# Two more output blocks ahead of the last retention head's scores, and two blocks of h read from PSUM at the end

## The chip, the core and the metric

The kernel runs on one core of a Trainium2 chip. The core has five engines with a queue of instructions each: TensorE (PE in the profile; its weight loads are shown apart as PEld), VectorE (DVE), ScalarE (ACT), GpSimd (POOL) and SyncE (SP), which here issues every transfer. An engine takes its queue in order; engines wait for each other by semaphores. The metric is device time in microseconds (us), the median over several executions.

## The reference

The reference is a decoder trunk with two layers over x of 1024 tokens x 1024 channels in fp32.

- Layer 0: `u = rms_norm(h)`; one projection gives q, k (4 heads x 256), v and a gate g (4 heads x 512). q and k are rotated. Retention runs in chunks of 128 tokens: per head `o = (q k^T * decay) v + (q * decay) state`, and `state = state * decay + (k * decay)^T v`. Each head's o is normalized over its 512 channels, multiplied by `silu(g)` and projected by `ret_w_out` (2048 to 1024). `h = x + rms_norm(y)`.
- Between the layers: `rms_norm(h) @ w_kv` gives one shared K (8 heads x 128) and V (8 heads x 256).
- Layer 1: q and gate from a projection of `rms_norm(h)`; stick-breaking attention (for each query, weights `sigmoid(z) * prod(1 - sigmoid(z))` over the later keys) over the shared K and V; gate, output projection, and again `h = h + rms_norm(y)`. The result is h.

## The kernel before

Activations lie transposed, channels on the 128 partitions and tokens along the free axis, in halves of 512 tokens, t=0 and t=1. Every fp32 matmul runs as three passes of a reduced fp32 form (`mm3`, L415 high by high, L416 high by low, L417 low by high). So each operand is first split: ACT writes the high part (L577, or L580 with a gain) and DVE the low part (L578, L581). Weights come by transfers into `wraw` (or other free tiles: `vo`, `ko`) and are split into `whl`, which has three buffers.

`run()` (L1493 to L1588) emits four phases in order: retention for t=0 and t=1 (class AHead, four heads u=0 to 3 each), then stick-breaking attention for t=0 and t=1 (CPair, four pairs of heads each), and `finish` at the end. A head of retention goes: projection of q and k; output projection of the head before (`last.out(yd)`, function `outproj`); scores (`H.scores()`); projection of v and g (`H.vg()`); and then, mixed into the next head's work, the product with v, normalization (L933 to L952), gate product (L979), transposes on PE (L983) and the split into `oT`, for the last head into `qk`.

The output projection is a list of 16 half chunks: eight blocks of 128 output channels, two halves each, 12 matmuls of 512 columns in a block. A block's sum goes to PSUM, DVE adds the sum so far (L517), and a transfer stores it to `y`. `go` and `merge` interleave such lists. For the last head (u=3) `run()` takes the first four half chunks ahead of the scores and holds the other twelve (`held`) to be emitted beside the head's tail. Its four first blocks use the PSUM tag `ma` alone.

PSUM has eight banks under the tags `ma`, `mb`, `z` and `o`, two buffers each. `banks4` (L390) is the usual alternation: ma, ma, mb, mb.

Within an engine the order is not that of the code. A planner (`arrange`, L101 to L305) takes the emitted steps with their reads and writes, and modelled costs, and orders each engine's queue anew. Two sets of a step bind it: `s.before`, steps of any engine that have to be planned earlier, and `s.behind`, the last reader on the same engine.

`finish` writes the last half (t=1) in two parts of 256 tokens, th=0 and th=1. `chunk` does a block: 12 matmuls, DVE adds the sum so far (L1442), ACT squares (L1444) and scales (L1445), DVE adds the square to `acc` (L1447). The last block's square stays in `box["q"]`. Then `col` sums over channels by matmuls with a column of `mean` (L1454, L1455), and POOL raises to the power -1/2 (L1458); `row` spreads the result over the partitions (L1464); `write` multiplies two blocks at once (L1470, k=0 to 3), adds h from the SBUF tile `A` (L1471) and stores. The additions of th=0 and the first of th=1 are on POOL, the three others of th=1 on DVE.

Of the kernel before, what the change touches and what calls it, by code (L numbers as in the profile page):

```python
# [15 lines left out]
AF = mybir.ActivationFunctionType  # L16
ALU = mybir.AluOpType
# [83 lines left out]
def arrange(nc, tc, tag_of, bufs, banks, turns):  # L101

    chip = Step()
    chip.banks = banks
    steps, last, users = [], defaultdict(list), defaultdict(list)
    for ins in nc.cur_bb.bb.instructions:
        s = Step()
        s.ins = [a.bass_ap for a in ins.ins if getattr(a, "bass_ap", None) is not None]
        s.outs = [a.bass_ap for a in ins.outs if getattr(a, "bass_ap", None) is not None]
        s.eng = str(ins.engine).split(".")[-1]  # L110
        if not s.outs or s.eng not in HAND:
            continue
        s.inst, s.op, s.k = ins, type(ins).__name__, len(steps)
        s.scan = bool(getattr(ins, "is_tensor_tensor_scan", False))
        s.turns = bool(getattr(ins, "is_transpose", False))
        s.before, s.after, s.behind, s.next = set(), set(), set(), set()
        reads = [(b.tensor.name, _cells(b)) for b in s.ins if type(b.tensor).__name__ == "Tile"]
        writes = [(b.tensor.name, _cells(b)) for b in s.outs if type(b.tensor).__name__ == "Tile"]
        for name, m in reads:
            s.before |= {o.k for o, n, w in last[name] if w and n & m}  # L120
            s.behind |= set([o.k for o, n, w in last[name] if not w and n & m and o.eng == s.eng][-1:])
        for name, m in writes:
            s.before |= {o.k for o, n, w in last[name] if n & m}
        for name, m in reads:
            last[name].append((s, m, False))
        for name, m in writes:
            last[name] = [z for z in last[name] if z[1] & ~m] + [(s, m, True)]
        s.tiles = sorted({name for name, _ in reads + writes})
        for name in s.tiles:
            users[name].append(s)  # L130
        s.before.discard(s.k)
        s.behind -= s.before | {s.k}
        for p in s.before:
            steps[p].after.add(s.k)
        for p in s.behind:
            steps[p].next.add(s.k)
        s.busy, s.whole = _time(s, chip)
        s.shares = s.eng == "Pool" or s.eng == "DVE" and sum(b.tensor.name not in banks for b in s.ins) > 1
        steps.append(s)
    at = {s.inst.name: s for s in steps}  # L140
    for a, z in turns:
        at[z].behind.add(at[a].k)
        at[a].next.add(at[z].k)
    tags = defaultdict(list)
    for name in sorted((n for n in users if n in tag_of), key=lambda n: users[n][0].k):
        tags[tag_of[name]].append(name)

    rank, best = latest(steps, users, tags, bufs), None
    for _ in range(5):
        end, order, follow = place(steps, users, tags, tag_of, bufs, rank)  # L150
        if best is None or end < best[0]:
            best = end, order
        rank = justify(steps, order, follow)
    order = best[1]
    edge = mybir.DependencyInfo(mybir.DependencyClass.NoSync, mybir.DependencyReason.DATA)
    for line in order.values():
        for a, b in zip(line, line[1:]):
            tc.add_manual_dep(steps[b].inst, steps[a].inst.name, edge, reason="order of the queue")
# [150 lines left out]
def trunk(ctx, tc, xT, wts, gains, trig, ident_in, cols, out):  # L309
# [11 lines left out]
    cnt, tag_of, banks, turns = [0], {}, set(), []  # L321
# [1091 lines left out]
    def finish(t, P, y_d):  # L1413
# [36 lines left out]
        def col(th):  # L1450
            p = PS("z")
            for b in range(2):
                o = 256 * th + 128 * b
                MM(p[:, b:b + 1], acc[:, o:o + 128], mean[:, 0:1], start=True, stop=False)  # L1454
                MM(p[:, b:b + 1], box["q"][:, 128 * b:128 * b + 128], mean[:, 0:1], start=False, stop=True)  # L1455
            ms, r = S("small", [2]), S("col", [4])
            V.tensor_scalar(ms[:], p[:, 0:2], EPS, None, ALU.add)
            G.tensor_tensor(r[:, 0:2], ms[:], mhalf[:, 0:2], ALU.pow)  # L1458
            box["r"] = r
# [6 lines left out]
        def write(th, k):  # L1466
            tl = slice(256 * th, 256 * th + 256)
            yy = f[:, 2 * k:2 * k + 2, tl]
            h = hs[k][:].rearrange("p (c t) -> p c t", c=2)[:, :, tl]
            V.tensor_tensor(yy, yy, box["row"][:, :256].unsqueeze(1).broadcast_to([128, 2, 256]), ALU.mult)  # L1470
            (G if th == 0 or k == 0 else V).tensor_tensor(yy, yy, h, ALU.add)  # L1471
            dma(out[256 * k:256 * k + 256, HT * t + 256 * th:HT * t + 256 * th + 256].rearrange("(c p) t -> p c t", c=2), yy)

        def post(th):
# [18 lines left out]
    def run():  # L1493
# [12 lines left out]
        for ip, (kind, t) in enumerate(phases):  # L1506
# [5 lines left out]
            for u in range(4):  # L1512
                ring[:] = rings(kind, t, u)
                if kind == "A":
                    H = AHead(t, u, X)
                    if u == 0 and ip == 0:
                        main = H.first_v(first)
                        load[0]()
                        for k in range(8):
                            main[2 * k]()  # L1520
                            if k == 0:
                                late_constants()
                            for n in load[3 * k + 1:3 * k + 4]:
                                n()
                            main[2 * k + 1]()
                            if k > 2:
                                norm[k - 3]()
                        go(H.qk(), lambda: [(norm[5:], 0, 4)])
                        go(H.first_g(), lambda H=H: [(H.scores(), 6, 0), (sums, 0, 6)])
                        H.nmix = 0  # L1530
                        last = H
                        continue
                    elif u == 0:
                        go(H.qk())
                    else:
                        n = 7 if ip == 0 and u == 1 else 8
                        go(H.qk(), lambda L=last, n=n: [(L.rest(), 0, n), (L.gate(), 18 - n, 2)])
                        held = last.out(yd, None, None if u < 3 else ("ma",) * 4)
                        go(held if u < 3 else held[:4],
                           lambda H=H, L=last, u=u, side=(pre if u == 2 and nxt[0] == "A" else post[:5] if u == 1 else post[7:10] if u == 2 else pre, 0, 2 if u < 3 else 0):  # L1540
                           [(L.give, 0, 12 if u < 3 else 0), side, (H.scores(), 5, 1) if u < 3 else ([], 0, 0)])
                        held = held[4:]
                    H.nmix = 3 if t else 2
                    go(H.vg(), lambda H=H, u=u, more=post[5:7] if u == 1 else post[10:] if u == 2 else []:
                       [([], 0, 0) if 0 < u < 3 else (H.scores(), 3, 15), (H.begin(), 20, 0), (more, 4, 8)])
                    last = H
# [111 lines left out]
```

## Time and profile before

| | |
|---|---|
| three executions | 1715.61, 1715.69, 1717.03 us; median 1715.69 |
| the profiled execution | 1716.91 us, its span 1714.8 us |
| PE busy | 1700.1 us, 99% of the span, 8057 matmuls |
| DVE, ACT, POOL busy | 1308.4, 880.9, 142.8 us |
| transfers | 348.78 MB, 203 GB/s on average |

The times in the profile's rows count from the start of the span, in us. A timeline row has start, duration, engine, line, operation, what it writes and reads, shapes, and in brackets how long the engine had been idle before, with the instruction that released it; `x4` is a run of four alike. Matmuls are pipelined: the distance of two starts, not the duration, is what a matmul costs. A row of windows has the stretch, its length, and the busy time of PE, weight loads, DVE, ACT and POOL, each with its count, then the granted clock of TensorE (1.00 is full), the share of the DMA engines and GB/s. A row of waits has the waiting engine, tile and line, what it waited for, and total, count and longest wait in us.

### The profile page before, as it was taken

To read this page: it belongs to the slowest core of one execution; us is meant where nothing else is said; L and a number is where in the kernel's file an instruction comes from. 1 tells how busy PE (TensorE), PEld (TensorE's weight loads), DVE (VectorE), ACT (ScalarE), POOL (GpSimd) and SP (SyncE) were. 2 spreads that over 40 slices of the span, in tenths; PEclk is the share of its full clock that TensorE was granted. 3 is DMA by queue.
4 is the path that set the end of the run, shared out by engine and by line. 5 is a ranking of instruction groups with operands and counts; after the bars stand their busy time and mean duration, and the time that the engine had idled before them with its cause. 6 is when DMAs were issued, how large, how long until landed. Compare 5 with 4: busy or idle time off the path is not lost.

```text
span 1714.8 us, 23975 instructions
## 1 busy us (share of the span) xinstructions
PE 1700.1 (99%) x8057; PEld 1419.0 (83%) x8057; DVE 1308.4 (76%) x2213; ACT 880.9 (51%) x1646; POOL 142.8 (8%) x275
## 2 busy tenths in 40 slices
PE   9999999999999999999999999999999999999997
PEld 7888888888888888878888888888888888888887
DVE  8856868889867978688888778667887756656865
ACT  6435536555545535355655544544674445445643
POOL 0000101010010000101010100000001001001001
PEclk9999999999999999999999999999999999999999
DMA  5236475668545676376896999667883763463523
GB/s 187 98 105 203 148 236 185 203 193 271 187 146 176 225 240 209 98 256 209 291 320 198 332 314 308 209 209 257 280 292 111 252 225 101 160 219 99 162 95 125
DMA packets 182250, 348.78 MB, mean 203 GB/s; under 512 B 20208, under 2 KB 24432, under 8 KB 182128
## 3 DMA queue, kind: packets, MB, share of 16 engines
q1 hardware_dynamic: 182128, 347.26, 61.0%
q8 instruction: 63, 1.03, 0.2%
q14 instruction: 59, 0.48, 0.1%
HBM read 273.78 MB, written 73.40 MB: 202 GB/s over the span
## 4 chain that ended last, share of the span: by engine, by line
PE 99%; DMA 0%; DVE 0%; ACT 0%; issue 0%; SPq 0%; POOL 0%; DVEq 0%
PE pmb L415 13%; PE pmb L417 13%; PE pmb L416 13%; PE pma L415 12%; PE pma L417 12%; PE pma L416 12%; PE po L417 5%; PE po L416 5%; PE po L415 5%; PE pz L1355 2%; PE pz L417 2%; PE pz L416 2%; PE pz L415 2%; PE pz L983 1%; PE pz L551 0%; DMA S<-in_xT_dram 0%
## 5 line engine op out<-in xcount | busy, mean ns | idle before, releaser
L577 ACT ACTIVATE whl<-wraw 128x512 fp32r<-128x512 f32 x323 | 190.8, 625 | 203.4 <-PE pmb L417 80.4
L578 DVE TENSOR_TENSOR whl<-wraw,whl 128x512 fp32r<-128x512 f32 x323 | 214.3, 686 | 64.3 <-ACT whl L577 63.1
L415 PE MATMUL pma<-xh,whl 128*128 128x512 f32 x384 | 153.1, 399 | 0.0
L415 PE MATMUL pmb<-xh,whl 128*128 128x512 f32 x384 | 152.4, 397 | 0.0
L417 PE MATMUL pma<-xh,whl 128*128 128x512 f32 x384 | 150.1, 391 | 0.0
L417 PE MATMUL pmb<-xh,whl 128*128 128x512 f32 x384 | 150.0, 391 | 0.0
L416 PE MATMUL pma<-xh,whl 128*128 128x512 f32 x384 | 149.9, 390 | 0.0
L416 PE MATMUL pmb<-xh,whl 128*128 128x512 f32 x384 | 149.6, 390 | 0.0
L1325 DVE TENSOR_TENSOR_SCAN sgn<-sgn 128x384 f32<-128x384 f32 (+4 forms) x64 | 86.5, 1354 | 27.7 <-POOL sgn L1323 27.7
L580 ACT ACTIVATE whl<-wraw,gn 128x256 fp32r<-128x256 f32 (+1 forms) x144 | 80.4, 600 | 50.0 <-PE pmb L417 32.4
L577 ACT ACTIVATE AT<-pz 128x512 fp32r<-128x512 f32 (+1 forms) x96 | 46.3, 487 | 108.0 <-PE pz L1355 105.9
L1322 POOL TENSOR_SCALAR_AFFINE_SELECT A<-A 128x128 f32<-128x128 f32 x64 | 33.1, 516 | 775.1 <-ACT A L1317 775.1
L578 DVE TENSOR_TENSOR AT<-pz,AT 128x512 fp32r<-128x512 f32 (+1 forms) x96 | 52.9, 555 | 57.6 <-ACT AT L577 57.1
L581 DVE SCALAR_TENSOR_TENSOR whl<-wraw,gn,whl 128x256 fp32r<-128x256 f32 (+1 forms) x144 | 82.0, 601 | 17.1 <-ACT whl L580 16.5
L415 PE MATMUL pmb<-oT,whl 128*128 128x512 f32 x240 | 94.9, 396 | 0.0
L417 PE MATMUL pmb<-oT,whl 128*128 128x512 f32 x240 | 93.8, 391 | 0.0
L416 PE MATMUL pmb<-oT,whl 128*128 128x512 f32 x240 | 93.7, 391 | 0.0
L577 ACT ACTIVATE whl<-S 128x512 fp32r<-128x512 f32 x104 | 63.0, 628 | 48.1 <-PE pmb L417 12.5
L417 PEld LDWEIGHTS pmb<-xh,whl 128*128 128x128 f32 x384 | 72.1, 188 | 15.8
L417 PEld LDWEIGHTS pma<-xh,whl 128*128 128x128 f32 x384 | 72.1, 188 | 15.6
L416 PEld LDWEIGHTS pmb<-xh,whl 128*128 128x128 f32 x384 | 72.2, 188 | 13.5
L415 PEld LDWEIGHTS pmb<-xh,whl 128*128 128x128 f32 x384 | 72.2, 188 | 13.4
(389 smaller groups left out, 4614.0 us busy)
## 6 DMA issues: line engine op xcount, KB each, us to landing
wraw<-in_wts_dram SPq DMA_DIRECT2D x522, 256.0 KB, 3.6
y<-f SPq DMA_DIRECT2D x120, 256.0 KB, 3.2
f<-y SPq DMA_DIRECT2D x88, 256.0 KB, 4.1
S<-in_wts_dram SPq DMA_DIRECT2D x44, 256.0 KB, 4.1
vo<-in_wts_dram SPq DMA_DIRECT2D x42, 256.0 KB, 4.3
ko<-in_wts_dram SPq DMA_DIRECT2D x40, 256.0 KB, 4.4
T<-AT SPq DMA_DIRECT2D x32, 256.0 KB, 4.7
sc<-T SPq DMA_DIRECT2D x16, 512.0 KB, 5.1
```

Of the source, the lines that this page charges most:

```text
L415: MM(p, lh, rh, start=start, stop=False, **kw)
L416: MM(p, lh, rl, start=False, stop=False, **kw)
L417: MM(p, ll, rh, start=False, stop=stop, **kw)
L577: A_.activation(dst[0], src, AF.Copy)
L578: V.tensor_tensor(dst[1], src, f32(dst[0]), ALU.subtract)
L580: A_.activation(dst[0], src, AF.Copy, scale=scale)
L581: V.scalar_tensor_tensor(dst[1], src, scale, f32(dst[0]), ALU.mult, ALU.subtract)
L983: nc.tensor.transpose(pt[:, 128 * e:128 * e + 128], on[:, 128 * e:128 * e + 128], ident[:])
L1322: first = G.affine_select(a[:, dg], a[:, dg], [[-1, 128]], ALU.is_gt, 0.0, base=0, channel_multiplier=1)
L1325: V.tensor_tensor_scan(n[:, :W][:, ::-1], n[:, :W][:, ::-1], n[:, :W][:, ::-1], 1.0, ALU.mult, ALU.bypass)
L1355: nc.tensor.transpose(p[:, 128 * tb:128 * tb + 128], self.A[hh][tb][:, c0:c0 + 128], ident[:])
```

## The change

There are four edits. In `arrange`, a read of a PSUM bank is also put behind the reads of that bank by other engines. For the last head, the output projection uses the usual alternation of banks, and eight half chunks instead of four are emitted ahead of the scores, for t=0 and t=1. In `finish`, `col` sums both columns over `acc` first and then both over `box["q"]`, as one accumulation; for th=1, two ACT copies bring the blocks k=2 and k=3 of h to two PSUM banks. In `write`, those two additions read h from PSUM, and POOL does three additions of th=0 (k=0 to 2) and two of th=1 (k=0, 1); the others are DVE's.

```diff
@@ -117,7 +117,7 @@  (arrange)
         for name, m in reads:
-            s.before |= {o.k for o, n, w in last[name] if w and n & m}
+            s.before |= {o.k for o, n, w in last[name] if n & m and (w or name in banks and o.eng != s.eng)}
             s.behind |= set([o.k for o, n, w in last[name] if not w and n & m and o.eng == s.eng][-1:])
@@ -1451,8 +1451,14 @@  (finish, col)
             p = PS("z")
             for b in range(2):
                 o = 256 * th + 128 * b
-                MM(p[:, b:b + 1], acc[:, o:o + 128], mean[:, 0:1], start=True, stop=False)
-                MM(p[:, b:b + 1], box["q"][:, 128 * b:128 * b + 128], mean[:, 0:1], start=False, stop=True)
+                MM(p[:, b:b + 1], acc[:, o:o + 128], mean[:, 0:1], start=b == 0, stop=False, skip_group_check=True)
+            for b in range(2):
+                MM(p[:, b:b + 1], box["q"][:, 128 * b:128 * b + 128], mean[:, 0:1], start=False, stop=b == 1, skip_group_check=True)
+            if th:
+                for k in (2, 3):
+                    box[k] = PS("ma")
+                    A_.activation(box[k][:].rearrange("p (c t) -> p c t", c=2),
+                                  hs[k][:].rearrange("p (c t) -> p c t", c=2)[:, :, 256:512], AF.Copy)
@@ -1468,7 +1474,9 @@  (finish, write)
             V.tensor_tensor(yy, yy, box["row"][:, :256].unsqueeze(1).broadcast_to([128, 2, 256]), ALU.mult)
-            (G if th == 0 or k == 0 else V).tensor_tensor(yy, yy, h, ALU.add)
+            if th and k > 1:
+                h = box[k][:].rearrange("p (c t) -> p c t", c=2)
+            (G if k < (2 if th else 3) else V).tensor_tensor(yy, yy, h, ALU.add)
@@ -1535,11 +1543,11 @@  (run)
-                        held = last.out(yd, None, None if u < 3 else ("ma",) * 4)
-                        go(held if u < 3 else held[:4],
+                        held = last.out(yd)
+                        go(held if u < 3 else held[:8],
...
-                        held = held[4:]
+                        held = held[8:]
```

The edits move instructions in the queues. The names in the rows are tiles with a number for each allocation; the sign <- stands between what is written and what is read, and brackets name the engines waited for. First PE's queue ahead of the scores of the last retention head, t=1. The scores are the matmuls into `pz` from `qk`; `pma`, `pmb` from `oT` are output blocks, L569 spreads a row of norm factors over the partitions, matmuls from `xh` belong to the projection of v and g. Before:

```order
L417 MATMUL pma_7094<-oT_6787,whl_7011 128x512
L569 MATMUL pz_7111<-sgn_7067,onesr 128x512 [waits DVE_49,PE_49]
L569 MATMUL pz_7111<-sgn_7067,onesr 128x512 [waits DVE_49]
L415 MATMUL pz_7187<-qk_6988 128x512 [waits PE_49,Activation_49]
L416 MATMUL pz_7187<-qk_6988 128x512 [waits DVE_49]
```

And with the change, where the first row is the end of the fourth block, and 36 matmuls of the projection stand from the fourth to the fifth of these rows:

```order
L417 MATMUL pmb_7137<-oT_6787,whl_7067 128x512
L569 MATMUL pz_7154<-sgn_7093,onesr 128x512 [waits DVE_49,PE_49]
L569 MATMUL pz_7154<-sgn_7093,onesr 128x512 [waits DVE_49]
L415 MATMUL pma_7168<-whl_7119,xh_3837 128x512 [waits DVE_49,Activation_49]
...
L417 MATMUL po_7217<-whl_7182,xh_3953 128x512
L415 MATMUL pz_7230<-qk_6988 128x512 [waits PE_49]
L416 MATMUL pz_7230<-qk_6988 128x512
```

The scores have moved behind more matmuls, and their waits for ACT and DVE are no longer written at these rows.

Second, PE's queue at the end of retention, t=1: the last transposes (L983) of the gated head, and the first matmul that reads the split of them (`qk`). Before:

```order
L417 MATMUL pma_7734<-oT_6787,whl_7624 128x512
L983 MATMUL pz_7760<-ident,sgn_7672 128x128 [waits DVE_49,PE_49]
L983 MATMUL pz_7760<-ident,sgn_7672 128x128 x3
L415 MATMUL pmb_7767<-oT_6787,whl_7725 128x512
...
L417 MATMUL pmb_7797<-oT_6787,whl_7725 128x512
L415 MATMUL pma_7815<-qk_7578,whl_7788 128x512 [waits Activation_49]
L416 MATMUL pma_7815<-qk_7578,whl_7788 128x512 [waits DVE_49]
```

With the change:

```order
L417 MATMUL pmb_7797<-oT_6787,whl_7705 128x512
L983 MATMUL pz_7757<-ident,sgn_7697 128x128 [waits DVE_49,PE_49]
L983 MATMUL pz_7757<-ident,sgn_7697 128x128 x3
L415 MATMUL pma_7815<-qk_7621,whl_7788 128x512 [waits Activation_49]
L416 MATMUL pma_7815<-qk_7621,whl_7788 128x512 [waits DVE_49]
```

The 24 matmuls of two output blocks that stood between the transposes and the readers are now ahead of the transposes or of the scores. On ACT the high part of these transposes has, with the change, this row of a weight copy in front of it:

```order
L952 ACTIVATE sgn_7697<-po_7667,small_7693,small_7692 128x512 [waits Pool_49]
L577 ACTIVATE whl_7896<-ko_7897 128x512 [waits DMAHW0_49,PE_49,Activation_49]
L577 ACTIVATE qk_7621<-pz_7757 128x4x128 [waits PE_49]
```

Before, a weight copy (`whl_7838<-vo_7839`, waiting for PE) stood there too; it is another one now.

Third, DVE's queue at the end. Before:

```order
L1442 TENSOR_TENSOR oT_16045<-pmb_16570,oT_16045 128x256 [waits PE_49]
L1442 TENSOR_TENSOR oT_16045<-pmb_16591,oT_16045 128x256 [waits PE_49]
L1447 TENSOR_TENSOR acc_16044<-acc_16044,f_16584 128x256 [waits Activation_49]
L1457 TENSOR_SCALAR small_16613<-pz_16608 128x2 [waits PE_49]
...
L1471 TENSOR_TENSOR oT_16045<-oT_16045,A_16171 128x2x256 [waits DVE_49]
L1471 TENSOR_TENSOR oT_16045<-oT_16045,A_16236 128x2x256 [waits DVE_49]
L1471 TENSOR_TENSOR oT_16045<-oT_16045,A_16292 128x2x256 [waits DMAHW4_49,DVE_49]
```

With the change (its lines 1463 and 1479 are 1457 and 1471 of before):

```order
L1442 TENSOR_TENSOR oT_16045<-pmb_16570,oT_16045 128x256 [waits PE_49]
L1479 TENSOR_TENSOR oT_16045<-oT_16045,A_16292 128x2x256 [waits DMAHW4_49,DVE_49]
L1447 TENSOR_TENSOR acc_16044<-acc_16044,f_16584 128x256 [waits Activation_49]
L1442 TENSOR_TENSOR oT_16045<-pmb_16591,oT_16045 128x256 [waits PE_49]
L1463 TENSOR_SCALAR small_16617<-pz_16608 128x2 [waits PE_49]
...
L1479 TENSOR_TENSOR oT_16045<-oT_16045,pma_16613 128x2x256 [waits DVE_49]
L1479 TENSOR_TENSOR oT_16045<-oT_16045,pma_16615 128x2x256 [waits DVE_49]
```

One addition of the first part now stands between the last two evacuations, the last addition to `acc` ahead of the last evacuation, and two additions of three are left at the end, from PSUM.

## The prediction

> **What bounds the kernel now.** I read the page first, then the list of TensorE's waits, then the timeline at each wait, then the granted clock by windows.
>
> ```profile
> span 1714.8 us, 23975 instructions
> PE 1700.1 (99%) x8057; PEld 1419.0 (83%) x8057; DVE 1308.4 (76%) x2213; ACT 880.9 (51%) x1646; POOL 142.8 (8%) x275
> PE 99%; DMA 0%; DVE 0%; ACT 0%; issue 0%; SPq 0%; POOL 0%; DVEq 0%
> ```
>
> TensorE (PE) is busy for 99% of the span, and 99% of the chain that ended last is PE. The change takes no matmul away, so it can only gain where PE stands still or after PE's last matmul. The whole list of PE's waits is five rows, engine and line, then what was waited for, total, count and longest in us:
>
> ```profile
> PE pz L415 <- ACT qk L577: 1.8, 1, 1.8
> PE pz L388 <- DVE f L386: 1.7, 1, 1.7
> PE pma L415 <- ACT oT L580: 1.2, 1, 1.2
> PE pz L1464 <- POOL col L1458: 1.0, 1, 1.0
> PE pz L1454 <- DVE acc L1447: 0.9, 1, 0.9
> ```
>
> Rows two and three are the start of the kernel, which the change does not touch. Rows four and five are in the end stage. Row one is the place of the first edit: the scores of the last retention head, second half of the sequence (t=1). The timeline there:
>
> ```profile
> 728.28 0.39 PE L417 MATMUL pma<-oT,whl 128*128 128x512 f32 x1
> ...
> 729.64 0.40 PE L417 MATMUL pma<-oT,whl 128*128 128x512 f32 x1
> 729.88 0.63 PE L569 MATMUL pz<-sgn,onesr 128*128 128x512 f32 x2
> ...
> 731.66 1.14 ACT L577 ACTIVATE qk<-f 128x512 fp32r<-128x512 f32 x2
> ...
> 732.33 0.50 PE L415 MATMUL pz<-qk 128*128 128x512 f32 x1 [1.82 <-ACT qk L577]
> ...
> 733.06 0.50 PE L417 MATMUL pz<-qk 128*128 128x512 f32 x1
> ...
> 734.17 0.52 PE L415 MATMUL pz<-qk 128*128 128x384 f32 x1
> ...
> 737.45 0.40 PE L416 MATMUL pma<-whl,xh 128*128 128x512 f32 x1
> ```
>
> The held output blocks end at 729.64, and PE stands until the high part of the rotated q and k is written. Between 728.28 and 729.64 lie six starts, so a 512-wide matmul takes 1.36/6 = 0.227 us of PE at full clock; a 384-wide one takes three quarters by width, 0.17. From 729.64 to 737.45 PE starts 13 wide and 5 narrow ones: 13 x 0.227 + 5 x 0.17 = 3.8 us of work in 7.81 us. So this place costs 4.0 us. Waiting alone does not make that up. Each row below is a window, its length, busy time of PE, weight loads, DVE, ACT and POOL, the granted clock, DMA share and GB/s; the first one is the third wait of the list:
>
> ```profile
> 6.94:10.36 3.42, 2.21 (x10) 1.34 (x9) 1.52 (x3) 1.69 (x4) 0.00 (x0) 1.00 0.97 310
> 730.57:733.98 3.41, 1.65 (x6) 1.09 (x7) 3.41 (x6) 2.23 (x5) 0.00 (x0) 1.00 0.63 227
> 733.98:737.39 3.41, 3.41 (x11) 3.01 (x10) 3.23 (x6) 0.60 (x1) 0.11 (x1) 0.50 0.87 288
> ```
>
> In the window in which PE worked 1.65 of 3.41 us the clock was still full; in the next it was half, which cost 3.41/2 = 1.7 us. Thus 4.0 = 2.3 of standing still (1.8 for the high part, the rest for the low one) + 1.7 of clock. Where PE worked 2.21 of 3.42 us the clock did not fall. Whether it falls thus depends on how a wait lies to the windows. I take that as the reason why the four executions shown stand in two groups, 1715.61 and 1715.69 against 1716.91 (this one) and 1717.03; their distance, 1.3, is near the 1.7.
>
> The Trainium skill, "TensorE: Matmul & The Clock Gate", Part 1, has a free-running window of 3413 ns, which agrees with the 3.41 us here; its table at the end asks for PE gaps above about 3 us before the clock falls, and here 1.8 us of idle did it, so the measurement decides. By the page's rule the 1.7 us would have come from elsewhere and no stall under 3 us in the changed kernel could lower the clock, so the second rival below would not exist.
>
> **Part 1, eight half chunks ahead of the scores.** Four output blocks (48 matmuls) instead of two (24) now precede the scores, and the order of the changed kernel also puts 36 matmuls of the next projection between the spreading of a norm row (L569) and the scores: 24 x 0.227 + 36 x 0.227 = 13.6 us of PE work where 2.3 were missing. The score's wait falls to nothing, and with it the half clock: -4.0 us against this execution, -2.3 us against one without the half clock. Cost elsewhere: banks mb stand in for ma, so the blocks' evacuations go by the alternation that every other output projection uses. I price that at nothing, covered by the 13.6 us.
>
> **What is late next.** The same matmuls are missing at the end of the head. Before, two whole blocks (24 matmuls, 5.4 us) stood between the last transposes (L983) and the first matmul that reads the transposed gate product (`qk`); in the changed order nothing does. At t=0 the recurrent state's matmuls stand there instead, and I find no such place. The chain at t=1 now, from the last matmul of the head's output, over batch statistics, normalization and gate product, to the transposes and their split:
>
> ```profile
> 792.41 0.39 PE L417 MATMUL po<-v,sc 128*128 128x512 f32 x1
> ...
> 792.91 0.70 DVE L933 BATCH_NORM_STATS2 small<-po 128x6 f32<-128x512 f32 x1 [1.69 <-PE po L417]
> ...
> 798.32 0.77 ACT L952 ACTIVATE sgn<-po,small,small 128x512 f32<-128x512 f32 x1
> ...
> 799.13 0.69 DVE L979 TENSOR_TENSOR sgn<-sgn,sg 128x512 f32<-128x512 f32 x1
> ...
> 800.84 0.60 PE L983 MATMUL pz<-ident,sgn 128*128 128x128 f32 x4
> ...
> 801.64 0.58 ACT L577 ACTIVATE qk<-pz 128x512 fp32r<-128x512 f32 x1
> ...
> 802.25 0.69 DVE L578 TENSOR_TENSOR qk<-pz,qk 128x512 fp32r<-128x512 f32 x1
> ```
>
> This takes 802.94 - 792.41 = 10.5 us, hidden today by PE work. The hand-off alone, where no queue delays it:
>
> ```profile
> 715.78 0.60 PE L983 MATMUL pz<-ident,sgn 128*128 128x128 f32 x4
> 716.14 0.47 PE L415 MATMUL pmb<-xh,whl 128*128 128x512 f32 x1
> 716.42 0.60 ACT L577 ACTIVATE oT<-pz 128x512 fp32r<-128x512 f32 x1 [2.66 <-PE pz L983]
> 717.05 0.69 DVE L578 TENSOR_TENSOR oT<-pz,oT 128x512 fp32r<-128x512 f32 x1 [2.48 <-ACT oT L577]
> ```
>
> From the transposes' start the high part is ready at 717.02 (1.24 us) and the low part at 717.74 (1.96 us). PE could go on 0.36 us after the transposes' start and would need the low part one matmul later, at 0.36 + 0.23 = 0.59 us. Missing: 1.96 - 0.59 = 1.4 us. In the changed ACT order a weight copy (`whl` from `ko`), which waits for the last matmul ahead of the transposes, stands right in front of the split: 0.6 us of work that starts some 0.25 us after the transposes do, so the split starts at 0.85 instead of 0.64, and the stall is 1.6 us. Bounds: the chain's own durations without its queueing are 0.5 (until 792.91) + 0.7 + about 1.3 for the small steps + 0.8 + 0.7 + 2.0 = 6 us, against 30 matmuls x 0.227 and three groups of transposes x 0.36 = 7.9 us that follow the head's output in the new order. So the last transposes are held by PE's own queue, not by the chain, and the hand-off decides: 1.4 is the lower bound. If the chain takes as long as measured, 10.5 against 7.9 + 0.6, it is 2.0 us. I take 1.6, nearest to the hand-off rows.
>
> **Part 2, the ends.** After PE's last large matmul the order is: last squares, column sums, power on POOL, broadcast (L1464), four multiplications, the additions of h, and the stores.
>
> ```profile
> 1697.87 5.60 POOL L1471 TENSOR_TENSOR oT<-oT,A 128x512 f32<-128x512 f32 x4 [1.75 <-DVE oT L1470]
> ...
> 1700.30 0.58 DVE L1447 TENSOR_TENSOR acc<-acc,f 128x256 f32<-128x256 f32 x1
> ...
> 1703.28 0.42 DVE L1442 TENSOR_TENSOR oT<-pmb,oT 128x256 f32<-128x256 f32 x1 [0.62 <-PE pmb L417]
> ...
> 1703.62 0.41 DVE L1447 TENSOR_TENSOR acc<-acc,f 128x256 f32<-128x256 f32 x1
> ...
> 1704.18 0.35 PE L1454 MATMUL pz<-mean,acc 128*128 128x1 f32 x2 [0.94 <-DVE acc L1447]
> ...
> 1707.03 2.48 DVE L1470 TENSOR_TENSOR oT<-oT,pz 128x512 f32<-128x512 f32 x4 [1.63 <-PE pz L1464]
> ...
> 1707.86 1.27 POOL L1471 TENSOR_TENSOR oT<-oT,A 128x512 f32<-128x512 f32 x1 [1.67 <-DVE oT L1470]
> ...
> 1709.43 1.89 DVE L1471 TENSOR_TENSOR oT<-oT,A 128x512 f32<-128x512 f32 x3
> ```
>
> DVE does four products and three additions, to 1711.32. Now it does two additions, each 1.89/3 = 0.63: it ends at 1710.7, and POOL's second addition, 1.27 after the first, at 1710.4. So the last store leaves about 0.6 us earlier. POOL did four additions in the first half of the tail and now three, with the fourth on DVE between 1702.7 and 1703.3, ahead of the last evacuation (L1442 at 1703.28). That last evacuation moves behind the addition to the sum of squares, so to about 1703.6, and the last square comes 0.3 us later; the column sums over `acc` now run first and need only two short matmuls after it, where four were left: 0.2 to 0.4 back by rows L1454's spacing of some 0.2. Net 0, between -0.3 and +0.3. The two copies of h to PSUM (ACT, 512 wide, 0.6 each by row 716.42) lie in ACT's free time between evacuations; if they delay the last squares the cost is up to 0.6. The part gives -0.55, bounds -0.8 and +0.5.
>
> Beside POOL the 256-wide addition took 0.58 us, and 0.41 once POOL was done: two engines on the same memory. The Trainium skill, "SBUF — State Buffer", section "Who interferes with whom", says that a DVE operation with two SBUF inputs contends with a POOL operation that reads SBUF, and these rows agree. By it DVE's additions that read h from PSUM would each cost 0.63 while POOL adds; with both inputs in SBUF they would cost up to 0.58/0.41 as much, which would take back 0.5 us.
>
> **The sum.** Against this execution: 1716.91 - 4.0 + 1.6 - 0.55 = 1714.0. Against the median, which is an execution of the faster group: 1715.69 - 2.3 + 1.6 - 0.55 = 1714.4. I say **1714.3**, own range 1713.4 to 1715.1.
>
> **Rivals.**
>
> 1. *The new stall also lowers the clock* (18%). 1.6 us of idle is about the 1.8 that did it in rows 730.57 and 733.98, while 1.2 in row 6.94 did not. Price +1.7: 1716.0, no gain at all.
> 2. *The half clock belongs to every execution of before* (14%): then the whole 4.0 is gained against the median too, and the two groups come from elsewhere. For it: this execution shows it, and 1.3 is not 1.7. Against it: one is all that I see. 1715.69 - 4.0 + 1.6 - 0.55 = 1712.7.
> 3. *The chain is held by the queues, slower than before* (6%). The place is ACT's and DVE's order ahead of the last split: one weight copy on ACT (0.6) and two low parts on DVE (2 x 0.7) in front of normalization and gate product push the transposes back by 2 us. Then the stall is 3.6 us and lasts long enough to halve the clock: 1714.4 + 2.0 + 1.7 = 1718.1. It decides from where stall and clock together exceed 2.3 + 0.55 = 2.85. For it: 10.5 us measured against 6 without queues. Against: PE now reaches the place later, and DVE's lead grows.
> 4. *The change does not do what it says* (5%): the scores still wait, because the projection ahead of them stalls on its own weights, whose low parts DVE must also write. DVE was busy 3.41 of 3.41 in row 730.57. Then the gain is 0 to 1 there, and the new stall and the ends remain: 1715.7 - 0.5 + 1.6 - 0.55 = 1716.2.
>
> **How the numbers follow.** The likeliest case has 57%. Its time is the forecast, 1714.3. The range reaches down to rival 2 and up to rivals 1 and 4: 1712.6 to 1716.3. What a measurement of this kernel can tell from no change is about 0.2%, 3.4 us: faster means below 1712.3, slower above 1719.1. Below 1712.3 lie the better part of rival 2 (7%), where the ends give 0.4 more, and 4% of the likeliest case, where the two places that I price at nothing give something: 0.11. Above 1719.1 lies only the far part of rival 3, with stalls that I have not seen: 0.04. Same: 0.85.
>
> **What would show it.** Right: no PE wait on `qk` at the scores (L415 into `pz`), full clock there, one new PE wait on ACT and DVE of 1.0 and 0.5 us at the first `pma` matmul from `qk`, DVE's last addition some 0.6 us closer to its last product's start. Wrong: a half clock behind the new wait (rival 1), a time near 1712.7 with a steady 1715.7 of the kernel before showing the half clock again (rival 2), a wait above 2.9 us (rival 3), waits on `whl` among the projection's matmuls (rival 4), or a last evacuation and square that come more than 0.3 us late.

## The result and the profile after

| | median of 22 executions | range |
|---|---|---|
| before | 1715.99 us | 1714.88 to 1717.94 |
| changed | 1713.53 us | 1711.98 to 1714.23 |

The ratio is 0.9985, with a 95% interval of 0.9978 to 0.9991: the changed kernel takes 2.5 us less, at least 1.5 and at most 3.8. That is a gain outside the noise, though below the 0.2% for which the prediction kept the word faster. The time lies in its range (1712.6 to 1716.3) and 0.8 us under its forecast of 1714.3.

The page of the changed kernel's profiled execution (1713.42 us) has these first lines:

```profile
span 1711.5 us, 23965 instructions
PE 1698.2 (99%) x8057; PEld 1418.0 (83%) x8057; DVE 1308.8 (76%) x2213; ACT 881.8 (52%) x1648; POOL 141.4 (8%) x275
```

Its list of TensorE's waits:

```profile
PE pz L388 <- DVE f L386: 1.7, 1, 1.7
PE pma L415 <- ACT oT L580: 1.3, 2, 0.7
PE pz L1470 <- POOL col L1464: 1.0, 1, 1.0
PE pma L415 <- ACT qk L577: 0.8, 1, 0.8
PE pz L1454 <- DVE acc L1447: 0.3, 1, 0.3
PE pma L416 <- DVE qk L578: 0.2, 1, 0.2
```

The wait of 1.8 us at the scores (into `pz`, from `qk`) is gone. Two new rows have come, both at the first output block that reads the last head's own `qk` (into `pma`). L1470 is the broadcast that was L1464. The wait for the last squares (L1454) has fallen from 0.9 to 0.3; it belongs to the ends. PE's busy time is 1.9 us lower with the same 8057 matmuls: that is the half clock, in which matmuls last longer. An execution of the kernel before that kept the full clock at the scores (e9_before below) has 1698.3 as well.

The scores' place, timeline of the changed kernel: the fourth block ends, the norm row is spread, and the projection goes on without a bracket, so without a wait.

```profile
734.37 0.40 PE L417 MATMUL pmb<-oT,whl 128*128 128x512 f32 x1
734.60 0.63 PE L569 MATMUL pz<-sgn,onesr 128*128 128x512 f32 x2
735.07 0.40 PE L415 MATMUL pma<-whl,xh 128*128 128x512 f32 x1
```

The new wait, in the timeline of the same execution:

```profile
800.05 0.68 DVE L979 TENSOR_TENSOR sgn<-sgn,sg 128x512 f32<-128x512 f32 x1
...
801.70 0.60 PE L983 MATMUL pz<-ident,sgn 128*128 128x128 f32 x4
...
801.95 0.63 ACT L577 ACTIVATE whl<-ko 128x512 fp32r<-128x512 f32 x1 [1.95 <-issue]
...
802.48 0.58 ACT L577 ACTIVATE qk<-pz 128x512 fp32r<-128x512 f32 x1
...
803.09 0.69 DVE L578 TENSOR_TENSOR qk<-pz,qk 128x512 fp32r<-128x512 f32 x1 [0.55 <-ACT qk L577]
803.11 0.50 PE L415 MATMUL pma<-qk,whl 128*128 128x512 f32 x1 [0.82 <-ACT qk L577]
...
803.84 0.50 PE L416 MATMUL pma<-qk,whl 128*128 128x512 f32 x1 [0.22 <-DVE qk L578]
804.17 0.39 PE L417 MATMUL pma<-qk,whl 128*128 128x512 f32 x1
804.40 0.39 PE L415 MATMUL pma<-qk,whl 128*128 128x512 f32 x1
```

Without a wait PE would have gone on at 801.70 + 0.36, and three matmuls later been at 802.74; it is at 804.40. That is 1.66 us. The gate product (L979) is done at 800.73, a microsecond before the transposes: they wait in PE's own queue, and what is missing is the hand-off over ACT and DVE, with the weight copy (`whl` from `ko`) in front of it on ACT.

When the matmuls of both traces are laid side by side, each counted from its trace's first, the changed kernel is ahead by 0.3 us at the 10th microsecond and 0.36 by the 200th, by 0.8 between 570 and 700, by 4.6 between 765 and 790, by 3.0 from 809 on, and by 3.2 at the last broadcast. So the scores' place gives 3.9 and the new wait takes 1.6. The 0.8 ahead of them are not the change's. The first 0.3 come from a transfer of x for which the first blocks wait: in the chain that ended last it lands at 8.75 before and at 8.44 here. The 0.3 to 0.4 near 565 us are found in e9_before too, the same kernel as before, so they belong to that one execution.

The last stage, first the last big matmul of each kernel, then the ends. Before:

```profile
1702.96 0.28 PE L417 MATMUL pmb<-qk,xh 128*128 128x256 f32 x1
...
1706.24 0.75 PE L1464 MATMUL pz<-ident,col 128*128 128x128 f32 x4 [1.04 <-POOL col L1458]
```

Changed:

```profile
1700.09 0.28 PE L417 MATMUL pmb<-qk,xh 128*128 128x256 f32 x1
...
1703.05 0.71 PE L1470 MATMUL pz<-ident,col 128*128 128x128 f32 x4 [1.04 <-POOL col L1464]
1703.80 2.48 DVE L1476 TENSOR_TENSOR oT<-oT,pz 128x512 f32<-128x512 f32 x4 [1.59 <-PE pz L1470]
1704.63 2.49 POOL L1479 TENSOR_TENSOR oT<-oT,A 128x512 f32<-128x512 f32 x2 [1.63 <-DVE oT L1476]
1706.20 1.27 DVE L1479 TENSOR_TENSOR oT<-oT,pma 128x512 f32<-128x512 f32 x2
```

Counted from the last big matmul, the broadcast comes after 3.28 us before and 2.96 now, the first of the four products (L1470 before, L1476 now) after 4.07 and 3.71, the last addition ends after 8.36 and 7.38, and the span (1714.75 and 1711.52 us, to two places) after 11.79 and 11.43. The last addition is 0.98 us earlier, the end only 0.36.

### The profile page after: what moved, and what is told of

Same layout as the page of the kernel before. It is cut to its first block, busy times and chain, and to the rows that moved or that the text cites. A ratio compares the mean times of both kernels' runs of the same rounds, so it can differ in the third digit from the quotient of the medians.

```text
span 1711.5 us, 23965 instructions
## 1 busy us (share of the span) xinstructions
PE 1698.2 (99%) x8057; PEld 1418.0 (83%) x8057; DVE 1308.8 (76%) x2213; ACT 881.8 (52%) x1648; POOL 141.4 (8%) x275
## 4 chain that ended last, share of the span: by engine, by line
PE 98%; DVE 1%; DMA 0%; ACT 0%; issue 0%; SPq 0%; POOL 0%; DVEq 0%
PE pmb L415 13%; PE pmb L417 13%; PE pmb L416 13%; PE pma L415 12%; PE pma L416 12%; PE pma L417 12%; PE po L417 5%; PE po L416 5%; PE po L415 5%; PE pz L1355 2%; PE pz L417 2%; PE pz L416 2%; PE pz L415 2%; PE pz L983 1%; PE pz L551 0%; DMA S<-in_xT_dram 0%
## 5 line engine op out<-in xcount | busy, mean ns | idle before, releaser
L580 ACT ACTIVATE whl<-wraw,gn 128x256 fp32r<-128x256 f32 (+1 forms) x144 | 80.4, 600 | 49.1 <-PE pmb L417 30.4
L415 PE MATMUL pmb<-oT,whl 128*128 128x512 f32 x256 | 101.3, 396 | 0.0
L417 PE MATMUL pmb<-oT,whl 128*128 128x512 f32 x256 | 100.1, 391 | 0.0
L416 PE MATMUL pmb<-oT,whl 128*128 128x512 f32 x256 | 100.1, 391 | 0.0
```

The lines of the kernel that those rows point to most:

```text
L415: MM(p, lh, rh, start=start, stop=False, **kw)
L416: MM(p, lh, rl, start=False, stop=False, **kw)
L417: MM(p, ll, rh, start=False, stop=stop, **kw)
L580: A_.activation(dst[0], src, AF.Copy, scale=scale)
```

## The experiments

Two theories had to be told apart first. The prediction's sum against the median, 1714.4, leaves 0.9 us of the gain open. Theory A: half of it and more sits at the scores, because the half clock hits many executions of the kernel before. Rival B: the ends give more than the 0.55 allowed.

**The head's edit alone (e1_heads).** The kernel before with the planner's rule and this edit:

```diff
-                        held = last.out(yd, None, None if u < 3 else ("ma",) * 4)
-                        go(held if u < 3 else held[:4],
+                        held = last.out(yd)
+                        go(held if u < 3 else held[:8],
...
-                        held = held[4:]
+                        held = held[8:]
```

> The kernel before with only the head's edit (eight half chunks and the usual banks, with the planner's new rule, without which the order of the queues locks up); the ends as before. Theory A (the gain sits at the scores, where the half clock hits most executions of the kernel before; the ends give 0.3 to 0.6): 1.9 to 2.2 us under the kernel before, no wait for qk at the scores, a new stall of 1.6 us at the first matmul that reads the transposed gate product. Rival B (the half clock is rare, 2.3 - 1.6 = 0.7 is all that the head's edit gives, and the ends give the rest): 0.6 to 1.0 us under the kernel before.

Measured: 1713.93 us against 1715.83, ratio 0.9989 (0.9980 to 0.9998), so 1.9 us less, theory A's number. The interval reaches from 0.3 to 3.4 us less, though, and so takes in rival B's 0.6 to 1.0 as well. The wait at the scores is gone, and the new one is there with the same two parts (0.8 and 0.2).

**The ends alone (e2_ends).** The changed kernel with the lines of `run()` put back.

> The kernel before with only the edits of the ends (column sums in the new order, two blocks of h through PSUM, additions dealt anew, and the planner's new rule). Theory A: 0.3 to 0.6 us under the kernel before, the wait of 1.8 us at the scores is still there. Rival B: 1.4 to 1.9 us under it.

Measured: 1715.09 against 1715.83, ratio 0.9996 (0.9987 to 1.0004): 0.7 us less, not clear of zero. The median is near theory A and outside rival B, but the interval, from 2.2 less to 0.7 more, takes in both. The two parts add up to 2.6, the whole change gives 2.5; with intervals this wide that is no proof. What speaks against rival B is in the traces: the ends move the span's end by 0.36, and the half clock is no rare case, as follows.

**The bank tags alone (e4_banks).** The kernel before, `held = last.out(yd)` with four half chunks as before.

> The kernel before with only the banks of the last head's output blocks changed (the usual alternation in place of ma alone), still four half chunks ahead of the scores. My theory: the wait at the scores stays at 1.8 us and the time within 0.6 us of the kernel before; it also shows a second time whether the clock halves behind that wait. Rival: the wait came from the banks (blocks that all use ma wait for their evacuation), then it is gone and the time is 2 us or more under the kernel before.

Measured: 1716.42, ratio 1.0001 (0.9992 to 1.0010), and the wait is 1.8 us as before. So it is not the banks.

**The clock, eight profiles with the same wait.** e4_banks, e2_ends, three runs below and two further executions of the kernel before keep the wait at the scores. Their profiles, with that of before, tell how often the clock halves. Two executions of the same kernel show both cases. The windows (columns as before) are laid on the edges at which the recorded clock changed. These edges stand whole windows of 3.413 us apart in all 14 profiles; in that of before, for instance, the clock becomes full at 6.94 and falls at 733.98, 213 windows later.

> The kernel before once more, for its clock. Of six profiles with the wait of 1.8 us at the scores so far three show a half clock behind it. Theory: where the wait lies whole within one window of 3.41 us (TensorE busy 1.6 of 3.41) the next window runs at half clock and the execution takes over 1715.7; where it is cut by a window's edge, the clock stays full and the execution takes less than that.

> As the run before, a further execution: wait whole in a window and half clock, or wait cut and full clock.

The first took 1714.00 us:

```profile
726.52:729.93 3.41, 2.23 (x10) 1.50 (x8) 3.41 (x7) 2.72 (x6) 0.00 (x0) 1.00 0.49 153
729.93:733.34 3.41, 2.77 (x12) 2.16 (x13) 3.41 (x7) 1.71 (x4) 0.00 (x0) 1.00 0.70 235
```

The second took 1717.39 us:

```profile
729.81:733.22 3.41, 1.59 (x6) 0.69 (x5) 3.41 (x6) 2.67 (x5) 0.00 (x0) 1.00 0.70 192
733.22:736.64 3.42, 3.42 (x11) 3.03 (x10) 3.42 (x7) 0.60 (x1) 0.00 (x0) 0.50 0.85 299
```

Where a window's edge cuts the wait, PE is busy 2.23 and 2.77 and the clock stays full; where one window holds it whole (1.59), the next one has half clock. Of the eight profiles four have the half clock: before (1716.91), e4_banks (1716.72), e8_deal (1715.78) and e10_before (1717.39). In all four one window holds the wait whole, with PE busy 1.59 to 1.65 us in it. Those without it are e2_ends (1713.41), e6_sbuf (1714.49), e7_col (1715.19) and e9_before (1714.00). In all four an edge cuts the wait. The closest case is e6_sbuf, where the wait is 729.52 to 731.34 and the edge lies at 729.75:

```profile
726.34:729.75 3.41, 3.18 (x14) 2.26 (x13) 3.41 (x7) 1.77 (x4) 0.00 (x0) 1.00 0.24 81
729.75:733.17 3.42, 1.83 (x7) 1.22 (x8) 3.42 (x7) 2.06 (x5) 0.00 (x0) 1.00 0.73 228
```

PE busy for 1.83 us of the window kept the full clock, 1.65 did not. So the place of the wait in the window explains all eight. It also gives the odds, as an estimate: if the edges lie anywhere alike, a wait of 1.82 us stays whole in a window of 3.41 in (3.41 - 1.82)/3.41 = 47% of executions; here it was four of eight. The bound between 1.65 and 1.83 is read at the scores alone. In the kernel's last microseconds, where the matmuls are narrower, the clock also fell behind windows with up to 2.24 us of busy PE (e2_ends, 1698.72 to 1702.14), so busy time alone is not the whole rule.

**Six half chunks in place of eight (e3_six).** The order has one block more than before ahead of the scores, and 7 matmuls behind the last transposes.

```diff
-                        go(held if u < 3 else held[:8],
+                        go(held if u < 3 else held[:6],
...
-                        held = held[8:]
+                        held = held[6:]
```

> The changed kernel with six half chunks ahead of the last head's scores and ten held back. In its order the scores follow three blocks directly, and 7 matmuls (7 x 0.227 = 1.6 us) stand behind the last transposes. My theory (both waits are a matter of how many matmuls stand there): the 1.6 us of the new stall go, the scores wait 0 to 0.8 us since 12 matmuls (2.7 us) cover the 2.3 that were missing, so 0.8 to 1.6 us under the changed kernel: 1711.9 to 1712.7 where that has 1713.5. Rival: the wait at the scores moves with the blocks, because DVE has to evacuate each block before it splits q and k; then the scores wait 1 us or more, the clock falls again, and the time is that of the changed kernel or above it.

Measured: 1713.75, ratio 0.9986 (0.9978 to 0.9995). The new wait is gone, as forecast, but the wait at the scores is 1.4 us, as the rival had it. Its other two signs are missing. The clock stays full behind this wait, with PE busy 2.05 us in the window that holds it. And it is not the blocks' evacuation (L517) that stands ahead of q and k, since that comes behind the scores. DVE's rows show what does: the third block needs a second weight tile, and its two low parts (`whl`) stand in front of the rotation of k (L719 to L722).

```profile
729.79 1.29 DVE L578 TENSOR_TENSOR whl<-wraw,whl 128x512 fp32r<-128x512 f32 x2 [0.24 <-ACT whl L577]
731.00 0.68 DVE L719 TENSOR_TENSOR f<-pmb,tab 128x512 f32<-128x512 f32 x1
...
732.80 0.68 DVE L722 TENSOR_TENSOR f<-f,f 128x512 f32<-128x512 f32 x1
...
733.60 0.50 PE L415 MATMUL pz<-qk 128*128 128x512 f32 x1 [1.36 <-ACT qk L577]
```

What is short at the scores is DVE's time, not a number of matmuls: a block that needs new weights gives PE 2.7 us of work and costs DVE 1.3 of them, besides 0.24 of idling for their high part. With eight the scores come behind the projection, and DVE has the whole time of 36 further matmuls.

**The tail earlier (e5_tail, e12_tail beside e11_after).** The changed kernel, with the last head's normalization and transposes emitted over the whole list of held blocks:

```diff
-            return self.rest() + self.gate(), 1, 4
+            return self.rest() + self.gate(), 0, 7
```

> The changed kernel with the last head's normalization, gate product and transposes emitted earlier beside the eight blocks that are held back (spread over the whole list from its first entry, in place of leaving four entries at the end). In its order 6 matmuls stand between the last transposes and their first reader, and the scores are where the changed kernel has them. My theory (the new stall of 1.55 us is the hand-off from PE to ACT and DVE and back, and 6 x 0.227 = 1.36 us cover it): the wait before the first reader falls to 0.2 to 0.4, the kernel takes 1.0 to 1.4 us less than the changed one: 1712.1 to 1712.5 where that has 1713.5. Rival: the chain of statistics, normalization and gate product is the limit, so the transposes themselves wait on DVE (L979) and the stall only moves: less than 0.5 us gained.

Measured: 1712.00 against 1715.94, ratio 0.9976 (0.9967 to 0.9986). Its whole list of PE's waits:

```profile
PE pz L388 <- DVE f L386: 1.7, 1, 1.7
PE pz L1470 <- POOL col L1464: 1.0, 1, 1.0
PE pma L415 <- ACT oT L580: 0.6, 1, 0.6
PE pz L1454 <- DVE acc L1447: 0.3, 1, 0.3
```

Neither `qk` wait is left: between the start and the column sums PE waits for nothing. The product of the last head is done at 798.90 and its transposes run at 799.72, so they still wait in PE's queue and not for the chain:

```profile
798.22 0.68 DVE L979 TENSOR_TENSOR sgn<-sgn,sg 128x512 f32<-128x512 f32 x1
...
799.72 0.60 PE L983 MATMUL pz<-ident,sgn 128*128 128x128 f32 x4
```

The rival, by which the stall would only move in front of the transposes, falls. The comparison beside the changed kernel on one chip:

> The changed kernel beside the next one on the same chip: 1713.5, and no half clock behind its new wait of 1.05 + 0.5 us, which has two parts with a matmul between.

> The kernel of e5 beside the changed kernel on the same chip: 1.3 to 1.6 us less than it, since the whole new wait is gone.

Measured: 1713.15 for the changed kernel, 0.9986 (0.9977 to 0.9995) of before, and 1712.31 for this one, 0.9978 (0.9969 to 0.9987). That is 0.8 us between the two medians, less than expected; in the first comparison it was 1.5 (1713.53 and 1712.00, from different series). The aligned traces give the place itself: from 790 to 812 us the changed kernel loses 1.6 us on the kernel before, e5_tail 0.1. The times of this kernel fall into two groups, some at 1710.5 to 1711.9 and some at 1712.3 to 1713.2. Two things differ between its two profiles: at the start, PE's wait for `oT` is 0.6 us in the one (1711.29) and 1.6 in the other (1712.78), and the last broadcast takes 0.71 us at full and 1.22 at half clock. It is the fastest kernel of the study, by 0.8 to 1.5 us against the changed one.

**The ends, taken apart (e6_sbuf, e7_col, e8_deal).** The three have the head of the kernel before and one execution each, so only the distances from the last big matmul are compared. These repeat well: the broadcast comes after 3.28 in all five profiles with the ends of before, and after 2.96 or 2.97 in all six with the new ends. e6_sbuf leaves out the two copies; DVE adds h from SBUF.

> The edits of the ends without the two copies to PSUM: DVE adds h from SBUF while POOL adds too. Counted from the start of the last big matmul: the changed kernel starts the last products 3.7 us later, ends the last addition 7.4 us later and the span 11.4 us later. Theory C (DVE and POOL hinder each other when both read two operands from SBUF): DVE's two last additions take 0.3 to 1.2 us more together, the last addition ends at 7.7 to 8.6. Rival D (no contention that counts): 7.4. If the last stores are what ends the kernel (theory S), the span's end moves by less than the additions do. The head's part is that of the kernel before, so this is also another look at whether the clock halves behind the wait at the scores.

```profile
1700.99 0.28 PE L417 MATMUL pmb<-qk,xh 128*128 128x256 f32 x1
...
1705.52 2.49 POOL L1472 TENSOR_TENSOR oT<-oT,A 128x512 f32<-128x512 f32 x2 [1.64 <-DVE oT L1471]
...
1707.09 2.07 DVE L1472 TENSOR_TENSOR oT<-oT,A 128x512 f32<-128x512 f32 x2
```

DVE's two additions take 2.07 us instead of 1.27, POOL's two take 2.49 as before. So theory C holds, with 0.8 us, and DVE is the one that waits. Reading SBUF is not dear in itself: in the kernel before, DVE's last three additions, all from SBUF and after POOL's, took 0.63 each (1.89 together). The last addition ends after 8.17, but the span after 1712.6 - 1700.99 = 11.6, 0.2 more than with the copies.

e7_col has only the new order of the column sums:

> The kernel before with only the new order of the column sums (both sums over acc, then both over the last square). From the start of the last big matmul the kernel before starts the last products after 4.07 us, the changed one after 3.71. If the order of the sums alone gives that, 3.7 here; if the new order of DVE's queue (the last addition to acc ahead of the last evacuation) gives it, 4.0 to 4.1. Also another look at the clock at the scores.

The clock fell during its broadcast (1.09 us instead of 0.7), so its products do not tell; the broadcast's start does. It comes 3.12 us after the last big matmul, halfway between 3.28 and 2.96. It is not DVE's order that is missing: here too the last addition to `acc` stands ahead of the last evacuation. But that addition is slower. The first row is e7_col's, the second the changed kernel's:

```profile
1700.95 0.62 DVE L1447 TENSOR_TENSOR acc<-acc,f 128x256 f32<-128x256 f32 x1 [0.48 <-ACT f L1444]
...
1700.16 0.41 DVE L1447 TENSOR_TENSOR acc<-acc,f 128x256 f32<-128x256 f32 x1
```

In e7_col POOL is still at its fourth addition of the first part (to 1701.28); in the changed kernel it has only three and is done at 1699.02. So the order of the sums, with the DVE order that follows from it, gives 0.16 us, and the new dealing of the first part's additions the other 0.16.

e8_deal deals the additions as before:

> The edits of the ends, but with the additions dealt as before (POOL all four of the first part and one of the last, DVE three of the last, two of these from PSUM). Theory S (with the additions done sooner, the last four stores of 256 KB pile up and their bandwidth ends the kernel): the last addition ends 0.6 us later than with the new dealing (8.0 after the start of the last big matmul), but the span ends only 0.0 to 0.3 us later (11.4 to 11.7). Rival E (the last addition sets the end): the span ends 0.6 us later, at 12.0. Also another look at the clock at the scores.

Here the broadcast comes after 3.14 and the addition to `acc` takes 0.62, as in e7_col. The broadcast ran at half clock (1.22). Beside e2_ends, from which it differs by the dealing alone and whose broadcast took 1.22 as well, the last addition ends after 8.67 instead of 7.89, 0.78 later. The span ends after 12.12 instead of 11.93, 0.19 later, and 0.18 of that are there already at the broadcast (3.14 and 2.96). So the later additions themselves cost the end nothing, and theory S holds. The windows of the changed kernel's last microseconds show what ends it; the two last columns are the share of the DMA engines and GB/s.

```profile
1706.80:1707.30 0.50, 0.00 (x0) 0.00 (x0) 0.50 (x2) 0.00 (x0) 0.32 (x1) 0.50 0.90 324
1707.30:1707.80 0.50, 0.00 (x0) 0.00 (x0) 0.17 (x1) 0.00 (x0) 0.00 (x0) 0.50 0.57 201
1707.80:1708.30 0.50, 0.00 (x0) 0.00 (x0) 0.00 (x0) 0.00 (x0) 0.00 (x0) 0.50 0.86 281
1708.30:1708.80 0.50, 0.00 (x0) 0.00 (x0) 0.00 (x0) 0.00 (x0) 0.00 (x0) 0.50 1.04 346
1708.80:1709.30 0.50, 0.00 (x0) 0.00 (x0) 0.00 (x0) 0.00 (x0) 0.00 (x0) 0.50 1.01 352
1709.30:1709.80 0.50, 0.00 (x0) 0.00 (x0) 0.00 (x0) 0.00 (x0) 0.00 (x0) 0.50 0.97 338
```

The four last stores are 1 MB. At 340 GB/s that is 3.1 us of transfers, and they ran from 1706.8 to 1710.3, with one dip between the first and the second store (0.57 in the second row) and then almost without a gap, while the last addition was done at 1707.47. From the start of the first of the four products to the span's end it is 7.7 us (7.71 to 7.73) in 13 of the 14 profiles, with either dealing. Only e6_sbuf has 7.9: there the second store is late, and the transfers almost stop ahead of it:

```profile
1708.50:1709.00 0.50, 0.00 (x0) 0.00 (x0) 0.50 (x2) 0.00 (x0) 0.00 (x0) 0.50 0.13 43
```

What sets the end is thus the first product; once the first two stores are out in time, bandwidth does the rest. Counted from the last big matmul the change brings the first product 0.36 us earlier: 0.16 by the order of the sums, 0.16 by the new dealing of the first part, and 0.04 since the clock fell during the broadcast in the one trace (0.75) and not in the other (0.71); e1_heads, with the ends of before and 0.71, has 4.03 instead of 4.07.

## Why the prediction was right, and where not

- *The scores.* Right in mechanism and size for the profiled execution: 4.0 forecast, 3.9 in the aligned traces. That cover is a matter of matmuls alone was too simple: e3_six gave one block more and still waited 1.4, because DVE, which also has to split the block's new weights, sets when q and k are ready. Eight works since the scores move behind the projection.
- *The new wait.* 1.6 forecast, 1.66 measured, at the place and with the two parts named. e5_tail shows the mechanism: the same transposes six matmuls earlier, and the wait is gone.
- *The half clock behind it (rival 1).* It did not come: neither in the profile of the changed kernel, nor in e1_heads, nor in e11_after. In the changed kernel one window holds the whole wait and PE still works 2.38 of 3.41 us in it:

```profile
800.72:804.14 3.42, 2.38 (x12) 1.58 (x11) 2.87 (x6) 1.63 (x3) 0.00 (x0) 1.00 0.74 241
```

  The rival, the first of the prediction's list (the one that its paragraph on the clock calls the second), rested on 1.6 us of idle being near to 1.8. But the new wait leaves PE idle for only 0.82 and 0.22 us, with a matmul between. At the scores, half clock followed 1.59 to 1.65 of 3.41 four times of four, and full clock 1.83 and more every time. The Trainium skill, "TensorE: Matmul & The Clock Gate", Part 1, has a free-running window. The same wait with and without half clock, and edges whole windows apart, agree with it. The advice in the last table of that page of the Trainium skill, no PE gaps above about 3 us, was too loose here: 1.8 us were enough.
- *The sum against the median: the term that was mis-sized.* The step that failed is "an execution of the faster group: 1715.69 - 2.3". I took the median as one without the half clock. In four of eight profiles it is there, so in the mean the scores' place costs 2.3 + 0.5 x 1.7 = 3.15, and the sum becomes 1715.69 - 3.15 + 1.6 - 0.55 = 1713.6; measured 1713.53. That it comes so near is in part luck: the 1715.69 was the median of three, and over 22 executions it is 1715.99. As gains, the sum of the prediction gives 1.3, the corrected one 2.1, and 2.5 (1.5 to 3.8) were measured. Rival 2 asked whether every execution has the half clock; the answer is one of two, and the truth lies between the two cases. The reading of two groups was right in kind: executions with it took 1715.8 to 1717.4, those without it 1713.4 to 1715.2, the kernels with changed ends counted in. But the 22 executions of the kernel before fill 1714.9 to 1717.9 without a gap, since their starts differ too (last section).
- *The ends.* -0.55 forecast; 0.36 in the traces, 0.7 (not clear of zero) in e2_ends. The sum was near, the working was not: I let the last addition's end carry over to the kernel's end. It came 0.98 us earlier, but the end follows the first product and the stores, so the term for the additions (0.6) is worth nothing at the end. I put the column sums at 0, with a last evacuation 0.3 us late. It came 0.07 late (its end 0.81 after the last big matmul instead of 0.74), and the broadcast came 0.32 earlier, half of it by the order of the sums and half because POOL no longer slowed the addition to `acc`.
- *The contention of DVE and POOL.* The up to 0.5 us that the prediction would have given back without the copies was 0.8 on DVE (2.07 against 1.27) and 0.2 at the end. The Trainium skill, "SBUF — State Buffer", section "Who interferes with whom", agrees in kind: a DVE operation with two SBUF inputs contends with a POOL operation that reads SBUF.

## What to carry to other kernels

Where cover is moved from one stall to another, look at what waits next at the place it is taken from, and at which engine really is late: here DVE's queue, which a block with new weights loads as well. A stall's price may be a mixture, since it lies differently to the clock's windows in each execution; take several profiles before a sum is made against a median, and lay the windows on the clock edges of the same trace, since 0.4 us beside them e6_sbuf would look like an exception. And before additions at the end are made faster, see whether the stores behind them already fill the transfer engines.

## What was not expected of the hardware

The kernels, alike at their start, begin at half clock (512-wide matmuls start 0.43 us apart, later 0.23), and the clock becomes full at a different time in each execution: between 4.55 and 7.87 us in the 14 profiles. Near the end the clock falls again at 1702 to 1707 us, in some executions during the last broadcast or ahead of it (0.71 us or 1.22).

It is not the start's clock, however, that spreads the start. The matmul that begins at 20.06 us in the profile of before, found by its number, begins between 18.5 and 20.2 in the 14 profiles. Among the three earliest is e8_deal (18.6), with the latest full clock of all (7.87), and e1_heads, with the earliest (4.55), comes at 19.8. What goes with it is PE's wait for the first normalized blocks (`oT`, L580). It is missing in the three earliest (e2_ends, e8_deal, e9_before) and 1.2 to 1.6 us at its longest in the three latest (before, e10_before, e12_tail). In before the chain to that wait runs through the transfer of x that lands at 8.75. These 1.7 us, the half clock at the scores and the clock in the last broadcast are of the size of the 3 us by which executions of the kernel before differ.

And the last 1 MB of stores took 3.4 to 3.6 us in every profile, whatever the additions ahead of it did.
